# A new order of issue on TensorE, VectorE and ScalarE, from the state-space stage to the feed-forward

## The chip, the cores and the metric

The kernel runs on one core of one Trainium2 chip. The metric is the time of one execution on the device in microseconds (us). The core's engines each work through their own stream of instructions: TensorE (PE, matrix products, with its weight loads, PEld), VectorE (DVE), ScalarE (ACT), GpSimd (POOL) and SyncE (SP), which here issues most of the transfers. An engine takes its instructions in the order of its stream, and each instruction waits until what it reads is written and what it overwrites has been read.

## The reference

One layer of a hybrid encoder trunk, in float32, for 512 frames of a new stream and 64 next frames of a running one with a past of 256. The width is 1024. A state-space branch (Mamba-2, 8 heads) and a latent attention branch (8 heads) stand side by side; their outputs are joined, projected and added to x, and a SwiGLU feed-forward of width 2816 follows.

```python
def hybrid_layer(x, ckv_past, krope_past, ssm_h0, conv_buf, p):
    proj = rmsnorm(x, p['norm_mix']) @ p['w_in']       # z, xbc, dt, q, ckv
    ...
    xbc, conv_new = causal_conv(xbc, conv_buf, p['conv_w'], p['conv_b'])
    y, h_new = ssd_scan(xh, dt, A, Bm, Cm, ssm_h0)     # chunked state-space scan
    y_ssd = rmsnorm((y + d_skip * xh) * silu(z), p['ssd_norm'])
    ...
    o_lat = mla_attend(q_lat, q_rope, q_pos, keys_c, keys_r, ...)
    o = jnp.einsum('bthl,lhd->bthd', o_lat, p['w_uv']).reshape(b, T, MLA_WIDTH)

    x = x + jnp.concatenate([y_ssd, o], axis=-1) @ p['w_out']
    hf = rmsnorm(x, p['norm_ffn'])
    x = x + (silu(hf @ p['w_gate']) * (hf @ p['w_up'])) @ p['w_down']
    return x, c_kv, k_rope, h_new, conv_new
```

The layer is run for both streams with shared weights; the outputs are the normed x of both, the new keys, the states and the last rows of the convolution.

## The kernel before

All 576 frames (512 + 64) lie along the free axis, in two halves of 288. The layer's channels lie on the 128 partitions, eight tiles of them. A float32 product is made of three products of split operands, high x high, high x low and low x high: for each block of weights ScalarE casts a high part (`split_weights`, L127, tiles wh_...) and VectorE subtracts it to get the low part (L128, wl_...). Most matmuls are 128x128 weights by 288 columns.

The stages, in the order of time: the input projection and convolution; the state-space scan in chunks (`chunk_a`, `chunk_e`: L520 to L552 hold the decays, for which SyncE loads rows into the tile ecp); the keys' value block (`ps_v`, L657, copied to V by ScalarE at L658); attention by pairs of heads, whose last product is pv (`values`, L771); the output projection (`out_tile`), in eight tiles t and two halves, first for the state-space half (cat_y) and last for the attention half (cat_o, steps O0 to O7), with the result added to x2 by VectorE (`evac`, L802); then the feed-forward.

The feed-forward's products are made by a seven-product scheme on 2 x 2 blocks. For each block of gate, up and down weights, `block_weights` loads two halves r2 and r1 (SyncE, L898 and L899; tiles gu_0 and gu_1, or db_0 and db_1), makes sums of them on VectorE (L901 to L904), casts (ScalarE, L906), splits the results (L127, L128), and last takes a low part (VectorE, L912, gu_a). `block_product` (L945) multiplies; its results go to the banks ps_x, ps_y and ps_z. Steps of the feed-forward's elementwise work (L1022 to L1034) and the operands of the down product (L1058 to L1065) run on VectorE in between.

Which slot of a pool a tile gets is fixed by strings of digits (`PLACES`), so a load can start only when the last reader of the slot's former tile is done. The order of work on each engine is written out by hand: `ISSUE` has one list for each engine. The numbers count the engine's instructions in the order in which the program creates them; the place in the list is the order in which the engine gets them. `issue_in_order` (L1342) chains each entry to the one ahead of it:

```python
for name, text in ISSUE.items():
    made = [i for i in nc.cur_bb.bb.instructions if i.engine == engines[name].engine]
    order = list(_places(text))
    for a, b in zip(order, order[1:]):
        tc.add_manual_dep(made[b], made[a].name, info, reason="issue order")
```

The instructions that the text speaks of by number:

| list | number | instruction |
|---|---|---|
| PE | 875 | first product of a value block, ps_v (L657) |
| PE | 1390-1403 | fourteen of the last products pv (L771) |
| PE | 1388-1389 | last two products of ps_o6_1, out-projection of tile 6 (L465) |
| PE | 1404 | first product of ps_o0_0, step O0 (L465); same bank as ps_o6_0 |
| PE | 1900 | product ps_z of block 3 with wl_gu_S (L945) |
| DVE | 366, 367 | x2[6] plus ps_o6_0, plus ps_o6_1 (L802) |
| DVE | 368, 369 | low part of cat_o, 64 and 512 columns (L764) |
| DVE | 375, 377 | first sums gu_2 of the first gate-up block, of gu_0 and of gu_1 (L901, L903) |
| DVE | 482, 495 | low parts gu_a of blocks 3 and 4 (L912) |
| DVE | 481 | low part wl_gu_S of block 3 (L128) |
| DVE | 489, 491 | sums of block 4 (L902, L904) |
| DVE | 466, 467, 468 | operands of the down product, pv (L1059, L1060, L1061) |
| DVE | 469, 474 | down operand fz (L1065), sum u from ps_x (L1026) |
| DVE | 518 | first sum of the first down block, db_2 of db_0 (L901) |
| ACT | 127, 142 | copy V from ps_v (L658), exponential of ecp (L552) |

Of the kernel before, what the change touches and what calls it, by code (L numbers as in the profile page):

```python
# [1390 lines left out]
142-147 152-171 174 270-271 175-177 272-274 178-187 172-173 188-269 275-367 373-383 368-370 384-419 421 420 422-455  # L1391
469-470 371 456-461 372 471-473 462-468 474-575 577 576 578-588 613-619 657 620-622 589-591 623-627 637-639 658 640
628-633 592-595 641 634 659-660 596-597 635-636 598-607 665 608-612 653 666-693 661 713 765 694-712 714-716 642-644
717-723 645-652 737 724 761 725 762-763 738 764 726 739-742 727-728 743 729 744 831-832 730-735 745-748 736 749-753
833 754-756 769 834 757-758 770-775 759-760 776-796 662-664 797-813 654 814-816 655-656 835-837 817-824 766-768 872
890-892 869 838 893 829-830 873-874 825-827 894 828 878 870-871 879 895 863-866 875-877 880 855-862 881-887 867-868
926-929 888 930-931 889 898 839-840 899 841-842 900-905 843-845 906-909 846-853 910-911 854 912-921 938 896 939 897
932-934 940 922-925 941-943 935-937 947-956 993 957-960 944-946 994-995 1012-1013 996-1001 1014 977-980 961-962
981-984 963-976 985-992 1015-1017 1002-1007 1018-1019 1008-1011 1020-1022 1024-1025 1028 1026-1027 1023 1063 1051 1035
1029-1030 1039-1041 1064-1065 1052 1036 1053 1032-1034 1042-1043 1054 1044 1031 1037 1066-1067 1055-1056 1068-1070  # L1400
1057-1062 1071-1073 1048 1074 1049-1050 1077-1082 1091-1093 1038 1045-1046 1094-1102 1047 1107-1109 1075 1110-1111
1076 1112 1083-1090 1129-1132 1123-1124 1103 1125 1133 1104 1134-1137 1126-1127 1138-1140 1128 1113 1106 1114-1115
1105 1141-1147 1153-1155 1148-1152 1169-1170 1116 1171 1117-1118 1172-1177 1121 1163 1178-1180 1159-1160 1156 1164
1119-1120 1193-1204 1181-1188 1289-1290 1122 1189-1192 1167 1291-1293 1157-1158 1277-1284 1161 1294-1296 1285-1288
1297 1168 1298-1301 1162 1302-1304 1206 1205 1305-1306 1165 1313-1316 1307-1308 1317 1309 1207 1166 1310 1318 1208
1319-1322 1311 1224 1312 1209 1225 1227 1323-1324 1226 1218-1223 1210-1217 1253-1254 1228-1231 1325-1326 1241 1237
1327-1328 1242 1329 1232 1330 1337 1243 1331 1338 1233-1236 1238-1239 1250-1251 1339 1252 1340-1342 1240 1244-1245
# [7 lines left out]
1685 1659-1661 1680 1666 1678-1679 1669 1706-1708 1681 1709 1670 1689 1710-1711 1676 1695 1690 1682 1667 1686 1696
1704 1701 1698 1687 1697 1688 1691 1699 1712-1717 1692-1694 1705 1742-1748 1730 1718-1723 1700 1724-1726 1731
1727-1728 1732-1734 1729 1702-1703 1735-1736 1749 1737-1741 1750 1766 1751 1754-1756 1767 1757-1764 1752-1753
1768-1770 1765 1771-1777 1790-1801 1778-1779 1826 1780 1827-1832 1802 1781 1833-1835 1782-1784 1803 1850 1785 1851
1814 1836 1786 1815 1852-1853 1787 1816-1817 1854 1788 1818-1821 1837 1855 1804 1856 1789 1857-1859 1805-1806
1822-1824 1860 1807 1861 1808-1812 1825 1910-1913 1813 1886-1887 1862 1914 1863 1915-1916 1888-1889 1838 1917-1918  # L1420
1839-1847 1864 1848-1849 1865-1866 1919 1890 1920 1867 1891 1868 1921 1892 1869 1893-1896 1870 1897 1874-1876
1898-1899 1877 1922-1929 1871 1930-1932 1878-1880 1900-1907 1933 1908-1909 1872-1873 1881-1885 1946 1934 1947
1935-1939 1958 1948 1959-1961 1940-1942 1949 1943 1950 1944-1945 1951-1953 1962 1954-1957 1970 1963 1971-1972
1964-1969 1994 1973-1976 1982-1983 1977 1995 1978-1981 1984 2018 1985-1986 1996-1997 2072 1998-2000 1987-1990
2001-2002 2006 2003 2007 1991-1992 2008 2019 2073 1993 2020 2004 2021 2009-2010 2074-2075 2024 2076-2077 2011
2025-2026 2022-2023 2005 2102 2027-2028 2012-2014 2060 2103 2029 2061 2090 2104-2105 2015-2016 2091 2030 2062-2063
2048-2049 2017 2106-2107 2092-2096 2064 2031 2050-2053 2108 2032 2036 2109-2110 2037 2097 2065 2054 2038 2033-2035
2055 2039 2056 2066-2068 2111-2112 2098-2101 2113 2069-2070 2040-2041 2057-2059 2132-2133 2071 2114-2120 2042 2078
2121 2079 2043 2134 2084 2080 2044 2085 2122 2045 2123 2086-2089 2124 2081 2125 2046 2135 2082 2047 2126-2129 2083
2162-2164 2136-2137 2165 2130 2166 2138-2140 2131 2141-2145 2150 2146 2167-2168 2151 2147 2152-2155 2148-2149 2186  # L1430
2156-2160 2169-2171 2174 2161 2175-2177 2172 2178-2181 2187 2173 2192 2188 2182-2185 2189 2240-2244 2190-2191
2193-2194 2245 2204 2195-2197 2205 2198-2199 2228 2216 2206-2207 2258 2208-2210 2229 2211 2200 2217-2219 2230
2220-2222 2212 2259-2260 2201 2213-2215 2264 2261 2265-2266 2223 2262-2263 2231 2224-2225 2267 2232 2270-2272 2226
2234 2227 2276 2268 2282 2269 2235-2236 2283 2237 2284 2238 2285 2277-2278 2239 2279-2281 2286 2246 2287 2273 2247
2252 2274 2288 2248 2289 2249 2253 2202-2203 2275 2250-2251 2233 2294 2254 2290 2300 2291-2293 2255 2295 2301-2302
2296 2318 2303 2256 2330 2304-2306 2331 2307-2308 2319-2320 2309 2332 2310-2312 2321 2333 2257 2313 2334 2314 2322
2315 2323 2316 2335 2317 2336-2337 2324 2338 2325 2297 2354 2339-2340 2342 2326 2343 2355 2327 2344 2328-2329
2345-2351 2341 2366-2367 2356 2352 2357-2358 2368 2353 2359 2298 2369-2371 2360-2361 2299 2362 2378 2363-2364 2379
2365 2380-2381 2372 2382-2383 2373-2374 2384 2402 2375 2414-2415 2385 2390 2386 2416-2418 2391 2387-2388 2419 2403
2376 2392-2396 2404 2397 2420 2389 2398-2400 2405 2421-2422 2406 2401 2438 2423 2407-2409 2424 2410-2411 2377  # L1440
2412-2413 2425-2430 2439-2441 2450-2451 2442 2452-2453 2431-2433 2443 2434 2454 2435 2455 2436-2437 2456 2444-2446
# [247 lines left out]
```

## Time and profile before

| | |
|---|---|
| median of 3 runs | 636.05 us (635.5 to 636.56) |
| profiled execution | 636.12 us |
| its span, first to last instruction | 634.1 us |
| granted clock of TensorE, mean | 0.998 |
| TensorE busy | 621.4 us (98%), 4717 matmul records |
| VectorE busy | 552.4 us (87%), 979 instructions |
| ScalarE busy | 388.5 us (61%), 749 instructions |
| GpSimd busy | 73.2 us (12%), 112 instructions |
| DMA, mean over the span | 118 GB/s |

The profiled execution's span is 2.0 us shorter than its time: that lies ahead of the first and behind the last instruction. In a row of a timeline the first number is the start, the second the length, then engine, line, operation, what is written and read, the shape and a count; a bracket at the end gives the idle time ahead of it and what ended it. A row of waits names who waited for whom, the total in us, how often, and the longest.

### The profile page before, as it was taken

The numbers are of one execution on the slowest core, as the hardware profiler recorded it, in microseconds if no ns is written. First come the engines' busy times: TensorE is split into PE (matmuls) and PEld (weight loads), VectorE is DVE, ScalarE is ACT, GpSimd is POOL, SyncE is SP. The second block draws the span as 40 slices with busy tenths as digits, with TensorE's granted clock in tenths as the row PEclk, the third lists the DMA queues.
The fourth block names the chain that finished last, engine by engine and source line by source line (L and its number), as shares of the span: only waits on it lengthen the run. The fifth ranks groups of instructions, "written<-read, shape, count | busy, mean of one in ns | idle before, by whom it ended". The sixth has DMA issues, their size and how long they took to land.

```text
span 634.1 us, 12124 instructions
## 1 busy us (share of the span) xinstructions
PE 621.4 (98%) x4717; PEld 593.8 (94%) x4717; DVE 552.4 (87%) x979; ACT 388.5 (61%) x749; POOL 73.2 (12%) x112
## 2 busy tenths in 40 slices
PE   9999999999999999999999999999999999999995
PEld 8899999977897899999999899999999999999994
DVE  6999897799867599999998897889888998999775
ACT  7653536599857379855656465655564666635464
POOL 1321141001010000000011002100111011100032
PEclk9999999999999999999999999999999999999999
DMA  8622184414221231223267436551666255734105
GB/s 297 222 47 83 35 212 119 141 62 142 107 77 34 97 104 65 79 61 131 56 155 186 125 96 154 140 139 51 177 150 155 67 164 119 167 101 159 47 0 184
DMA packets 32889, 74.64 MB, mean 118 GB/s; under 512 B 3882, under 2 KB 11960, under 8 KB 32576
## 3 DMA queue, kind: packets, MB, share of 16 engines
q1 hardware_dynamic: 26688, 62.73, 30.6%
q0 software_dynamic: 5424, 10.57, 9.4%
q8 instruction: 37, 0.61, 0.4%
q10 hardware_dynamic: 720, 0.57, 0.3%
q14 instruction: 20, 0.16, 0.1%
HBM read 59.14 MB, written 4.15 MB: 100 GB/s over the span
## 4 chain that ended last, share of the span: by engine, by line
PE 86%; DMA 5%; DVE 4%; ACT 3%; issue 1%; SPq 0%; DVEq 0%; ACTq 0%
PE ps_x L945 20%; PE ps_z L945 10%; PE ps_dx L1085 9%; PE ps_in L143 8%; PE ps_o L465 5%; PE ps_y L945 5%; PE ps_dz L1085 4%; PE ps_l L1155 4%; PE sc L724 3%; PE ps_first L143 2%; PE ps_dy L1085 2%; PE ps_z L465 2%; DMA gu<-in_w_gu 2%; PE ps_p L945 2%; PE ptp L746 1%; PE pv L771 1%
## 5 line engine op out<-in xcount | busy, mean ns | idle before, releaser
L945 PE MATMUL ps_x<-xop,wh_gu_S 128*128 128x288 f32 x504 | 122.5, 295 | 0.0
L945 PEld LDWEIGHTS ps_x<-xop,wh_gu_S 128*128 128x128 f32 x504 | 87.0, 188 | 0.3 <-DVE u L1026 0.3
L945 PE MATMUL ps_x<-xop,wl_gu_S 128*128 128x288 f32 x252 | 73.7, 295 | 1.6 <-DVE wl_gu_S L128 1.6
L945 PE MATMUL ps_z<-xop,gu_a 128*128 128x288 f32 x252 | 61.7, 295 | 0.0
L127 ACT CAST wh_gu_S<-gu 128x1024 fp32r<-128x1024 f32 x44 | 46.0, 1053 | 15.2 <-PE ps_y L945 4.3
L128 DVE TENSOR_TENSOR wl_gu_S<-gu,wh_gu_S 128x1024 fp32r<-128x1024 f32 x44 | 53.0, 1219 | 0.9 <-ACT wh_gu_S L127 0.5
L945 PEld LDWEIGHTS ps_x<-xop,wl_gu_S 128*128 128x128 f32 x252 | 47.2, 188 | 1.8 <-DVE wl_gu_S L128 1.8
L1098 POOL DMA_DIRECT2D x<-db x16 | 14.8, 927 | 279.1 <-ACT dc L1091 169.5
L143 PE MATMUL ps_in<-xs,wh_in 128*128 128x288 f32 x256 | 45.5, 298 | 0.0
L945 PE MATMUL ps_y<-xop,wh_gu_A 128*128 128x288 f32 x168 | 44.7, 296 | 0.0
L945 PEld LDWEIGHTS ps_z<-xop,gu_a 128*128 128x128 f32 x252 | 43.5, 188 | 0.0
L945 PE MATMUL ps_x<-xop,wh_gu_A 128*128 128x288 f32 x168 | 42.9, 295 | 0.0
L945 PE MATMUL ps_z<-xop,wh_gu_S 128*128 128x288 f32 x168 | 42.1, 295 | 0.0
L143 PEld LDWEIGHTS ps_in<-xs,wh_in 128*128 128x128 f32 x256 | 37.8, 188 | 0.2
L127 ACT CAST wh_gu_A<-gu 128x1024 fp32r<-128x1024 f32 x22 | 23.1, 1050 | 16.7 <-PE ps_x L945 13.6
L128 DVE TENSOR_TENSOR wl_gu_A<-gu,wh_gu_A 128x1024 fp32r<-128x1024 f32 x22 | 26.8, 1219 | 4.2 <-ACT wh_gu_A L127 2.9
L945 PEld LDWEIGHTS ps_y<-xop,wh_gu_A 128*128 128x128 f32 x168 | 30.2, 188 | 0.1
L465 PE MATMUL ps_o<-cat_y,wh_out 128*128 128x288 f32 x128 | 29.9, 317 | 0.0
L945 PEld LDWEIGHTS ps_x<-xop,wh_gu_A 128*128 128x128 f32 x168 | 29.6, 188 | 0.0
L945 PEld LDWEIGHTS ps_z<-xop,wh_gu_S 128*128 128x128 f32 x168 | 29.2, 188 | 0.0
L143 PE MATMUL ps_in<-xs,wl_in 128*128 128x288 f32 x128 | 27.8, 296 | 0.0
L465 PE MATMUL ps_o<-cat_o,wh_out 128*128 128x288 f32 x128 | 27.4, 300 | 0.3 <-ACT ps_o L462 0.3
(609 smaller groups left out, 1997.2 us busy)
## 6 DMA issues: line engine op xcount, KB each, us to landing
gu<-in_w_gu SPq DMA_DIRECT2D x44, 512.0 KB, 4.9
db<-in_w_down SPq DMA_DIRECT2D x16, 512.0 KB, 3.9
x<-db POOLq DMA_DIRECT2D x16, 288.0 KB, 6.5
x<-dc POOLq DMA_DIRECT2D x16, 288.0 KB, 4.0
wr_in<-in_w_in SPq DMA_DIRECT2D x8, 512.0 KB, 6.3
wr_out<-in_w_out SPq DMA_DIRECT2D x8, 512.0 KB, 3.2
cumb<-cumD SPq DMA_DIRECT2D x5, 512.0 KB, 4.6
x<-in_xT SPq DMA_DIRECT2D x2, 1152.0 KB, 5.6
```

Source lines behind the costliest of these rows:

```text
L127: act.copy(hi, raw)
L128: dve.tensor_tensor(lo, raw, hi.bitcast(F32), ALU.subtract)
L143: pe.matmul(ps[:m, hf, :n], w, x[:, hf * n : (hf + 1) * n], start=start and k == 0 and i == 0, stop=stop and k == last and i == 2,)
L465: pe.matmul(ps[:, :n], w, x[:, cols], start=not onto and k == 0 and i == 0, stop=onto or (k == len(terms) - 1 and i == 2), skip_group_chec ...
L724: pe.matmul(s[:, :nk], qs[:, j, q0 : q0 + P], ks[:, j, :nk], start=True, stop=True)
L746: pe.transpose(pp[:, k : k + P], prs[p, i][:, j, b * P : b * P + P], ident)
L771: pe.matmul(pv[64 * j : 64 * j + 64, b * P :], V[b][:, h * HD : (h + 1) * HD], pts[p, b, j], start=b == 0, stop=True, skip_group_check=b > 0,)
L945: pe.matmul(ps, p, q, start=not onto and first and kp == kps[0] and j == 0, stop=onto or (last and kp == kps[-1] and j == 2), skip_group_c ...
L1085: pe.matmul(ps, l, r, start=not onto and k == 0 and j == 0, stop=onto or (k == n - 1 and j == 2), skip_group_check=onto,)
L1098: pool.dma_start(x2[t], v, accum_op=ALU.add)
L1155: pe.matmul(ps, w, x[:, cols], start=first and not onto and k == 0 and i == 0, stop=onto or (last and k == len(terms) - 1 and i == 2), ski ...
```

## The change

Only the lists `ISSUE["PE"]`, `ISSUE["DVE"]` and `ISSUE["ACT"]` are written anew. Those of GpSimd and SyncE stay, as do the instructions themselves, their operands, and the slots of `PLACES`. In the list of TensorE 1515 of 4431 places hold another instruction than before, in VectorE's 373 of 979, in ScalarE's 285 of 718; they run from 58 us (the end of the input projection) to 338 us (the first down blocks) of the profile. The lists are the same before and behind that. In each engine's stretch the same numbers occur, in another order.

```diff
     "PE": """
...
-1343 1332-1333 1246 1334-1336 1247 1276 1248-1249 1275 1263-1268 1255-1262 1269-1271 1366-1367 1272-1274 1368-1371
-1344 1349-1353 1355 1354 1345 1356 1346 1357-1358 1347 1372 1363-1364 1359-1361 1348 1365 1362 1373-1376 1378-1381
-1390-1403 1382 1377 1383-1389 1404-1486 1488-1489 1487 1490-1509 1629 1512 1510-1511 1513-1523 1632 1620 1524-1534
...
-1898-1899 1877 1922-1929 1871 1930-1932 1878-1880 1900-1907 1933 1908-1909 1872-1873 1881-1885 1946 1934 1947
...
+1276 1251-1252 1247-1249 1275 1263-1268 1255-1262 1269-1271 1366 1272 1347-1348 1367-1368 1273 1369 1274 1349-1351
+1370-1372 1352-1354 1373-1374 1355-1357 1375-1377 1358 1363-1365 1378-1380 1359-1362 1381-1387 1390-1403 1388-1389
+1404-1426 1428-1431 1427 1432-1496 1500 1497-1498 1501 1499 1502-1504 1632 1626 1505-1509 1512-1515 1510-1511
...
+1849 1862 1911-1919 1888-1892 1863-1865 1893-1896 1866 1897 1920-1921 1874-1877 1922-1931 1898-1899 1878-1883 1934
+1932 1884 1867-1869 1885 1870 1900-1903 1871 1904-1908 1872-1873 1935 1933 1936 1909 1937-1942 1946-1947 1943-1945
...
     "DVE": """
...
-335 328 327 339 337 336 331-332 342 338 345 361 343-344 340 351-352 346 349 353 341 347 354 348 350 363 362 365 364
-366 369 367 383 368 375 371 382 372 377 376 378-380 373 381 374 386 398 384 388 387 385 389 409 394 391 390 395
...
-453 440 460 452 441 477 459 479 442 478 488 476 463 435 462 443 480 465 464 473 490 470 482 474 495 467 466 481 489
-469 518 491 471 486 492 487 520 484 519 493-494 468 483 485 496-497 522 498 503 499 532 521 534 501 472 502 523 504
...
+350 363 362 365 364 375 377 366 368-369 367 383 371 380 372 382 378 376 379 373 381 386 390 374 398 384 388-389 387
...
+458 433-434 440 461 441 453 452 442 459-460 488 435 476 443 479 477 473 463 462 465 478 480 464 489 466 490 470 482
+474 518 495 467 491 468 481 492 484 494 469 483 487 486 485 520 499 497 493 471 496 519 498 503 501 522 504 500 521
...
     "ACT": """
...
-116 99 84 96 98 104 80 126 97 78 100 103 101 93 105 102 115 114 110 109 107 112 122 95 108 156 91 113 111 117 138 137
-163 106 140 135 141 139 119 121 128 142 136 123 134 143 127 120 208 129 124 130-132 152 147-148 154 151 145 157 133
...
+141 134 140 106 138 119 137 121 127 139 163 128 143 123-124 129 120 208 130-131 146 152 148-149 132 145 154 133 157
+150-151 147 142 125 144 210 155 153 158-159 162 160-161 118 168 164-165 170-171 166 178 172 179 169 167 184 174-175
...
```

More of the change, by code (lines that the diff above doesn't have):

```diff
@@ L1395 @@
[L1395 to L1404, printed above, removed]
@@ L1415 @@
[L1415 to L1419, printed above, removed]
@@ L1425 @@
[L1425 to L1429, printed above, removed]
@@ new lines @@
+1173 1154-1155 1174-1180 1121 1193 1167 1194 1181 1195-1196 1182-1183 1197-1203 1156 1122 1163 1184-1186 1204 1164
+1187 1157 1159-1161 1205 1289-1291 1162 1292-1294 1188 1168 1158 1295-1296 1189-1190 1165 1191-1192 1297-1300 1224
+1277 1207-1208 1278-1280 1209 1281-1282 1206 1166 1313 1283 1314-1315 1284-1287 1316 1288 1317-1319 1225 1301 1320
+1302-1307 1227 1321-1322 1308-1312 1323-1324 1226 1237 1218-1223 1210-1217 1253-1254 1228-1231 1236 1325-1326
+1232-1233 1327-1328 1337 1238-1239 1241 1240 1242-1243 1234-1235 1329-1335 1338-1341 1244-1246 1342-1346 1336 1250
@@ new lines @@
+1648 1584-1595 1653 1596-1604 1649 1608 1605 1643 1606 1609 1607 1668 1610-1619 1654-1655 1669 1638 1650-1652
+1662-1664 1645 1671 1656-1657 1646 1665 1674 1683-1684 1675 1685 1658 1639 1677-1678 1666-1667 1670 1689 1676 1690
+1706-1708 1672 1640 1679 1709-1710 1673 1695 1692 1659 1696 1691 1711-1714 1686 1704 1687 1715 1688 1716 1693
+1660-1661 1680 1717 1698-1699 1681 1700 1694 1682 1697 1705 1742 1718 1701 1743 1719-1721 1730 1744 1722-1724 1745
+1725 1746-1747 1731 1726-1729 1702 1732-1739 1703 1748-1751 1740 1752 1754 1741 1755-1756 1766 1753 1757-1765
@@ new lines @@
+2085 2118 2086-2087 2119-2120 2078-2080 2133 2121-2123 2044-2047 2088 2124 2134 2125-2127 2135-2136 2089 2081 2128
+2082-2083 2137-2140 2129-2131 2141-2144 2162 2150-2151 2145-2147 2163-2169 2240 2148-2149 2241 2152-2153 2170-2171
+2154-2155 2186-2187 2156 2242-2243 2157-2159 2188 2160-2161 2172 2244 2189 2245 2173-2180 2190 2181-2184 2192 2191
+2193 2185 2194-2196 2258 2270-2271 2197 2259 2198-2199 2216 2204-2208 2217 2222 2209-2211 2228 2212-2215 2223 2218
+2260 2219 2261-2262 2220-2221 2272 2200-2202 2229-2230 2263-2267 2224 2273 2234 2225 2235-2236 2282 2237-2238
@@ new lines @@
+2402 2375 2414-2415 2385 2390 2386 2416-2418 2391 2387-2388 2419 2403 2376 2392-2396 2404 2397 2420 2389 2398-2400
+2405 2421-2422 2406 2401 2438 2423 2407-2409 2424 2410-2411 2377 2412-2413 2425-2430 2439-2441 2450-2451 2442
+2452-2453 2431-2433 2443 2434 2454 2435 2455 2436-2437 2456 2444-2446 2457 2447-2448 2458 2449 2462-2466 2486 2459
+2467-2468 2474-2476 2469 2477 2470 2498 2460 2471-2472 2499 2487 2478-2479 2461 2500 2488 2480 2473 2501 2489-2490
+2481 2491-2492 2482 2493 2483 2494 2484 2495 2485 2502 2576 2522 2496 2577 2503-2505 2578 2497 2579-2580 2523-2524
@@ new lines @@
+2510 2525 2581 2506-2507 2511-2512 2526-2527 2513-2514 2528 2606 2515 2529 2516-2519 2530 2520-2521 2531 2564 2607
+2532-2533 2508 2534 2509 2535 2540 2565 2541 2608 2566 2594 2552 2542 2536 2567 2600 2543-2545 2601 2553 2568 2595
+2554-2555 2569 2596 2546-2547 2597 2537 2548 2558 2549 2556 2550 2598-2599 2609 2538 2557 2602 2551 2559 2539 2603
+2560-2561 2610-2611 2562-2563 2618 2570-2571 2619 2572 2604 2573 2612 2574-2575 2605 2582-2583 2613 2620 2614-2617
+2588 2630-2632 2621 2589 2622 2590 2633 2623-2624 2584-2587 2636 2625 2637 2634 2626-2627 2638 2591 2628-2629
@@ new lines @@
+2639-2640 2654-2657 2592 2658 2642-2643 2593 2641 2635 2644-2645 2659-2661 2646 2666 2647-2649 2667 2662 2650
+2663-2665 2668 2651-2652 2669 2653 2670 2690 2671-2672 2696-2697 2673 2691 2698 2678 2674 2679-2680 2675 2681-2685
+2692 2676-2677 2686-2687 2744 2699-2700 2688-2689 2745-2747 2701-2702 2693-2695 2748 2708-2711 2703 2712-2713 2726
+2714 2727 2749 2732 2715 2704 2733-2734 2716 2720 2717 2721 2705 2722-2723 2762 2718 2774 2763 2724 2706 2728 2725
+2764 2729 2719 2768 2735 2765 2769 2775 2730 2738 2766 2739 2731 2740 2776-2777 2707 2741-2742 2786 2743 2770 2767
@@ new lines @@
+2906-2907 2894-2895 2918 2889 2908-2909 2919 2890-2892 2910 2896-2898 2911 2879-2880 2899 2893 2900 2912-2913
+2901-2902 2914 2881 2903 2915 2904-2905 2920 2916 2921-2923 2917 2942-2943 2924 2930-2935 2944-2945 2936 2954 2925
+2955 2926 2946-2947 2937 2948 2927 2938 2928-2929 2956 2949-2951 2939 2952 2940 2953 2957 2941 2958-2963 2978
+2964-2969 2990 2970-2971 2979 2972-2975 2980 2976-2977 2981 3002 2982 2991 2983 3003 2992 3004 2984 2993-2995 2985
+2996 3005 2997 2986 2998 3006 3080 2999-3001 3007 3081 3008 2987 3082 2988 3009 3026-3028 2989 3029 3010-3011 3083
@@ new lines @@
+3390 3413 3391-3392 3414 3384 3398 3393-3394 3415 3395 3422 3396 3423 3399 3424 3416 3397 3400 3425 3401 3417
+3402-3405 3446 3418 3406 3426 3447 3407-3408 3427-3430 3419 3385 3420 3409 3448-3449 3421 3431-3433 3450-3453
+3434-3437 3454 3438-3439 3458 3455 3440-3442 3456-3457 3459 3443-3445 3460-3464 3482 3465 3506 3466 3470 3467
+3471-3472 3483 3473 3468 3474-3476 3507 3494 3477 3484 3495 3478 3508 3479-3481 3485 3496 3486-3487 3469 3488 3497
+3489-3492 3498-3499 3493 3500 3509 3530 3501 3510 3502 3531 3511 3518 3503 3519-3520 3504 3512 3532 3584 3521 3513
@@ new lines @@
+3522 3505 3585 3514 3523-3524 3533 3515 3534 3525 3535 3586 3526 3516 3587 3527 3536 3517 3528 3588 3529 3589 3537
+3572 3538 3573 3539-3541 3560 3574 3542 3548 3602 3549 3543-3544 3561-3562 3545 3550-3551 3603-3604 3563 3552-3553
+3614 3564-3565 3615 3554-3557 3546 3575 3547 3608 3578 3566 3576-3577 3567 3609 3579 3605 3558 3568 3616 3610
+3569-3570 3559 3571 3580 3617 3606 3618 3581-3582 3607 3611-3612 3590 3626 3591 3583 3592 3627 3620 3613 3621
+3593-3594 3622 3628 3623 3629 3624-3625 3630 3595 3638 3631 3639 3596 3619 3632-3633 3640-3641 3597 3634-3636
@@ L1518 @@
+4319 4337-4338 4320-4321 4339-4340 4323 4341 4324 4342 4325 4343 4326 4344 4327 4371 4359 4328-4329 4348-4349 4345
+4330-4331 4358 4350 4383-4384 4351 4372 4352-4353 4332 4354 4360 4333 4355 4361 4373-4374 4385 4356 4375-4376 4395
+4357 4386 4396 4387-4388 4362-4363 4389 4364 4397 4365-4366 4377-4378 4367 4379 4398 4368 4399 4380 4369 4390 4400
+4391 4401 4370 4392 4381 4393 4382 4394 4402 4407 4403-4406 4408-4430
 """,
@@ L1552 @@
+947 946 948-949 951 956 952 950 954-955 953 958 960-961 964-965 957 959 962 966 963 967-978
 """,
@@ L1578 @@
+713-714 717 716 715
 """,
```

268 lines of the change are left out of this document (118 added, 150 removed).

## The prediction

> **What bounds the kernel now.** I read the page's busy times first, then TensorE's waits in the stretch whose order changes (58.7 to 338 us), then its windows, and last the timelines around the few places that stood out.
>
> ```profile
> span 634.1 us, 12124 instructions
> PE 621.4 (98%) x4717; PEld 593.8 (94%) x4717; DVE 552.4 (87%) x979; ACT 388.5 (61%) x749; POOL 73.2 (12%) x112
> ```
>
> ```profile
> PE ps_v L657 <- ACT V L658: 1.5, 1, 1.5
> PE ps_o L465 <- ACT ps_o L462: 0.3, 1, 0.3
> PE ps_p L945 <- ACT xop L877: 0.2, 1, 0.2
> ```
>
> ```profile
> 90.00:145.00 55.00, 53.48 (x473) 48.28 (x472) 45.33 (x88) 36.86 (x94) 9.44 (x13) 1.00 0.38 110
> ...
> 218.00:262.00 44.00, 43.52 (x317) 42.18 (x316) 41.68 (x73) 35.20 (x62) 0.00 (x0) 1.00 0.33 116
> 262.00:338.00 76.00, 76.00 (x574) 76.00 (x574) 74.79 (x121) 47.10 (x80) 4.41 (x5) 1.00 0.36 102
> ```
>
> TensorE is busy 98% of the span; in the changed stretch it waits three times, 2.0 us in all. That is the ceiling of any gain, since the diff moves instructions and removes none. The columns are the stretch, its length, the busy time of TensorE, its weight loads, VectorE, ScalarE and GpSimd with their instructions, the granted clock, and the share and rate of the DMA. The last stretch has no idle TensorE at all, and gives its cadence: 76.00 us for 574 matmuls, 0.132 us each. VectorE is nearly as full: 74.79 of 76.00 us. So what a new order on VectorE makes wait, it can't catch up soon, and TensorE has no slack of its own to give.
>
> **How the lists are read.** VectorE has 979 recorded instructions and its list 979 entries, so the n-th row is the n-th entry; the numbers below were put on the rows so. An engine stands at an entry until its inputs are there. What counts is therefore where an entry that needs a late input now stands ahead of one that TensorE needs.
>
> **Part 1: the state-space stage.** One wait of 1.5 us, at the first product of a latent value block:
>
> ```profile
> 126.19 0.63 ACT L552 ACTIVATE ecp<-ecp 128x512 f32<-128x512 f32 x1 [1.79 <-DMA ecp<-cumD]
> 127.68 0.57 ACT L658 COPY V<-ps_v 128x512 f32<-128x512 f32 x1
> 128.30 0.50 PE L657 MATMUL ps_v<-wh_uv,ckv 128*128 128x512 f32 x1 [1.52 <-ACT V L658]
> ```
>
> ScalarE stands 1.79 us for a load into ecp, with the copy V queued five instructions behind it; TensorE needs that copy. The new ScalarE list has the copy (127) at place 130 instead of 136 and the exponential of ecp (142) at 154 instead of 131, so the copy no longer stands behind the load. The wait goes, 1.5 us. What is late next: the new lists put TensorE's ps_v ten places earlier and the first out-projection product five places earlier, against inputs that come when they came. Bounds: nothing is won (a wait of the same size moves on), or 2.0 with every small wait gone. I take 1.5 less three earlier matmul places that nothing covers, 3 x 0.132 = 0.4, since 0.132 each is the nearest row: **-1.1**.
>
> **Part 2: the attention stage's end and the first gate-up block.** VectorE's list read `365 364 366 369 367 383 368 375 371 382 372 377`; it now reads `365 364 375 377 366 368 369 367 383 371 380`. 366 adds the finished ps_o6_0 to x2 (L802) and so empties its bank; 375 (L901) and 377 (L903) are sums for the first gate-up block, of the loads issued at L898 and L899. TensorE's product 1404, the first of O0, writes the bank that 366 empties.
>
> ```profile
> 217.33 0.46 DVE L802 TENSOR_TENSOR x<-ps_o,x 128x288 f32<-128x288 f32 x1 [3.19 <-PE ps_o L465]
> 219.98 0.69 DVE L901 TENSOR_TENSOR gu<-gu 128x512 f32<-128x512 f32 x1
> 221.92 0.68 DVE L903 TENSOR_TENSOR gu<-gu,gu 128x512 f32<-128x512 f32 x1
> ```
>
> ```profile
> 216.75 0.41 PE L465 MATMUL ps_o<-cat_y,wh_out 128*128 128x288 f32 x1
> 216.99 0.43 PE L465 MATMUL ps_o<-cat_y,wl_out 128*128 128x288 f32 x2
> 218.06 0.42 PE L465 MATMUL ps_o<-cat_o,wh_out 128*128 128x288 f32 x2
> ```
>
> ```profile
> 216.21 0.33 SPq L898 DMA_DIRECT2D gu<-in_w_gu  x1
> 216.59 0.43 SPq L899 DMA_DIRECT2D gu<-in_w_gu  x1
> ```
>
> ```profile
> SPq L898 <- PE pv L771: 20.5, 1, 20.5
> ```
>
> ```profile
> 220.03 0.62 ACT L906 CAST gu_a<-gu 128x512 fp32r<-128x512 f32 x1 [2.58 <-DMA gu<-in_w_gu]
> ```
>
> ```profile
> gu<-in_w_gu SPq DMA_DIRECT2D x2, 512.0 KB, 4.2
> ```
>
> SyncE waits 20.5 us for the last product pv, whose operand lies in the place that the load fills; in the new TensorE list seven of the nine products of ps_o6 that stood between pv (1390-1403) and O0 go ahead of pv, two stay behind it. TensorE's work ahead of O0 is the same, but pv, and with it the load, comes 7 x 0.13 nearer to O0. I keep pv's end, so 216.21, as the fixed point. ScalarE, which stood 2.58 us for it, starts at 220.03: it lands at about 220.0. The median of both from issue to landing is 4.2; with 3.8 for the first, the second took 4.6 and lands at 216.59 + 4.6 = 221.2. Then: 375 from 220.0 to 220.7; 377 from 221.2 to 221.9 (its 0.68); 366 starts 0.08 before that end, as rows behind each other do, and takes 0.46: 222.3, with 0.05 to TensorE 222.33. TensorE, which had nine matmuls from 216.75 to 218.06, now has two to do behind pv and is ready for O0 at 216.75 + 0.24 + 0.13 = 217.12. A wait of **+5.2**, where there was none (O0 began at 218.06, straight behind the nine). Bounds: 0.6 less if the second load takes the first one's 3.8 (377 then starts behind 375), and 0.8 more if it takes that spread longer than reckoned: 4.6 to 6.0. Behind 366 on VectorE stand 368, 369 (the low part of cat_o, due ten matmuls into O0, 1.3 us) and 367; they end within 1.0 us of 366 and cost nothing.
>
> **Part 3: between the two blocks.** The other two waits of the view, 0.3 and 0.2, lie in the moved stretch behind O0, and TensorE's delay there lets the copies that it waited for finish: **-0.5**. Bounds: 0 and -0.5.
>
> **Part 4: the first down block.** VectorE's list read `482 474 495 467 466 481 489 469 518 491`; it now reads `489 466 490 470 482 474 518 495 467 491 468 481`. 482 (L912) is the last reader of a buffer that the first load for down goes to; 518 (L901) is the first sum of that load; 481 (L128) makes the low part of the weights S3 and S4 of block 3, which TensorE's product 1900 reads.
>
> ```profile
> 283.12 0.69 DVE L912 TENSOR_TENSOR gu_a<-gu,gu_a 128x512 fp32r<-128x512 f32 x1
> 283.72 0.46 DVE L1026 TENSOR_TENSOR u<-ps_x,u 128x288 f32<-128x288 f32 x1
> 284.24 0.69 DVE L912 TENSOR_TENSOR gu_a<-gu,gu_a 128x512 fp32r<-128x512 f32 x1
> 284.85 0.45 DVE L1060 TENSOR_TENSOR pv<-u,pv 128x288 f32<-128x288 f32 x1
> 285.22 0.45 DVE L1059 TENSOR_TENSOR pv<-u,u 128x288 f32<-128x288 f32 x1
> 285.59 1.22 DVE L128 TENSOR_TENSOR wl_gu_S<-gu,wh_gu_S 128x1024 fp32r<-128x1024 f32 x1
> 286.73 0.69 DVE L902 TENSOR_TENSOR gu<-gu,gu 128x512 f32<-128x512 f32 x1
> 287.70 0.69 DVE L901 TENSOR_TENSOR db<-db 128x512 f32<-128x512 f32 x1
> 288.30 0.68 DVE L904 TENSOR_TENSOR gu<-gu,gu 128x512 f32<-128x512 f32 x1
> ...
> 295.27 0.45 DVE L1061 TENSOR_TENSOR pv<-u,pv 128x288 f32<-128x288 f32 x1
> ```
>
> ```profile
> 283.87 0.38 SPq L898 DMA_DIRECT2D db<-in_w_down  x1
> ```
>
> ```profile
> SPq L898 <- DVE gu_a L912: 14.1, 1, 14.1
> ```
>
> ```profile
> db<-in_w_down SPq DMA_DIRECT2D x1, 512.0 KB, 3.7
> ```
>
> ```profile
> 288.57 0.29 PE L945 MATMUL ps_z<-xop,wl_gu_S 128*128 128x288 f32 x1
> ```
>
> The load leaves 0.07 behind the end of 482 (283.80) and lands 3.7 later. In before, the seven instructions from 474 to 469 cover that, and 518 starts at 287.70 without a wait. Now only 474 (0.46) stands between, so VectorE stands some 3.3 us. From the end of 482 to that of 481: 3.81 to the landing, then 518, 495, 467, 491, 468 and 481 by the distances of their rows, 0.60 + 0.61 + 0.37 + 0.60 + 0.37 + 1.22, together 7.58. Before it was 286.81 - 283.80 = 3.01. So 481 is later by 4.57, and by 0.97 more since 489 (0.60) and 466 (0.37) now stand ahead of 482. TensorE reads it five matmuls later, -0.66, and had slack: 288.57 - 286.81 less 0.05 is 1.71. That leaves 3.2; VectorE's little idle ahead (1.2 of 76 us) takes up some 0.3: **+2.9**. Bounds: 0.3, if TensorE read it ten matmuls later instead of five and all of VectorE's idle (1.2) and both moved sums (0.97) were hidden; 3.7, the whole landing.
>
> **Part 5: the rest.** About 1500 other entries of TensorE, 340 of VectorE and 280 of ScalarE change places. The same instructions run; what hides them is the 0.132 cadence of TensorE with its inputs ready, as the stretch from 262 to 338 shows. Price if that cover goes: as the waits above. I take 0, with 1 us either way for the range. From 338 us on all lists are the same. SyncE's and GpSimd's lists don't change, but SyncE's two loads stand as reckoned above.
>
> **The sum.** -1.1 + 5.2 - 0.5 + 2.9 = +6.5. The profiled execution took 636.12 us (span 634.1 and 2.0 around it), 0.07 above the median of 636.05, so 642.6 against that execution and **642.5 us** against the median.
>
> **The rivals.** The first: after standing for 5 us TensorE runs slowly for a while.
>
> ```profile
> 1.06 3.78 PE L218 MATMUL ps_warm<-ones 128*128 128x128 f32 x16 [1.06 <-POOL nepsb L110]
> 5.32 2.07 PE L143 MATMUL ps_first<-xs,wh_first 128*128 128x288 f32 x9 [0.47 <-ACT xs L157]
> ```
>
> At the start nine matmuls go from 5.32 to 7.23, 0.212 each against 0.132. A share of 0.38 is lost, over 1.9 us of this row alone or 6.2 from the first matmul: 0.7 to 2.3. I take 1.9, once, behind wait 2 (the other is shorter): **644.4 us**. For it: the start. Against it: no idle of TensorE in this stretch is over 1.5 us, and the one at 128.30 lies in a stretch (90 to 145) with a clock of 1.00, so these rows can't decide. The Trainium skill, "TensorE: Matmul & The Clock Gate", section "Why this matters for your kernels", states that a gap of more than some 3 us between bursts takes the clock to half; by that rule it would happen behind wait 2, while for wait 4 the gap is too near to say.
>
> The second: only one of the two waits appears. Wait 2 alone (the down load lands under cover, VectorE being so late that the load is there): 636.05 - 1.6 + 5.2 = **639.6**. Wait 4 alone (366 isn't what O0 needs first): 636.05 - 1.6 + 2.9 = **637.3**.
>
> The third, on the other side: VectorE reaches 375 so late that both loads have landed, because it is behind by the time it leaves 364, and likewise at 518. Then only the early gain stays: 636.05 - 1.6 = **634.4**. It decides if VectorE comes to 375 after 221.2 instead of some 214; that is 7 us of delay, of which the rows show none: VectorE stood 3.19 us idle ahead of 366. The fourth: the lists don't tell in time, since TensorE had only 2.0 us to lose and inputs come early enough: 636.
>
> **How the numbers follow.** Both waits, as summed: 0.50, own range 640.5 to 644. Slow clock behind them: 0.20. Wait 2 alone 0.08, wait 4 alone 0.06. Faster 0.10, no change 0.06. About 0.2%, 1.3 us, is what a measurement can tell from no change: faster is under 634.8, slower over 637.3. Wait 4 alone lies on that edge and is halved: same 0.09, slower 0.81, faster 0.10. Leaving out the two fastest cases, 0.16, the range begins at 637.0; it ends at 646.0, the forecast with the clock's 2.3 and 1.2 of the upper bounds above (0.8 and 0.8, not both in full).
>
> **What would show it.** Wait 2: a row of L802 on VectorE behind the two sums, idle on a load at the first, and a TensorE wait of ps_o on x (L802) of 5 us. Wait 4: VectorE idle of 3 us ahead of the first db sum, and a TensorE wait on wl_gu_S (L128) of 3 us. Part 1: no wait on V. The clock: a granted clock under 1.00 in the window behind wait 2. Wrong would be the sum if pv came earlier against the rest, or if the landing of either load were shorter by more than a microsecond.

## The result, and the profile after

The changed kernel takes 647.08 us (median of 6 runs, 644.91 to 647.5) against 636.05 us (6 runs, 635.5 to 636.56): a ratio of 1.0167, interval 1.0152 to 1.0182. That is 11.0 us slower, where 6.5 had been forecast and 646.0 was the end of the range. The profiled execution took 646.19 us, 10.1 more than the one shown of before, with a granted clock of 0.991 instead of 0.998.

The busy times of the page of after, and TensorE's waits from 50 to 350 us (who waited for whom, total, times, longest):

```profile
span 644.3 us, 12133 instructions
PE 624.5 (97%) x4717; PEld 594.9 (92%) x4717; DVE 553.9 (86%) x979; ACT 388.2 (60%) x749; POOL 72.9 (11%) x112
```

```profile
PE ps_o L465 <- DVE x L802: 5.2, 1, 5.2
PE ps_z L945 <- DVE wl_gu_S L128: 2.8, 1, 2.8
PE ps_b L536 <- DVE bc L413: 1.1, 1, 1.1
PE ps_y L573 <- ACT R L640: 0.3, 1, 0.3
PE ps_z L465 <- DVE zh L476: 0.2, 1, 0.2
```

The two large waits are those that the prediction reckoned at 5.2 and 2.9 us; they came out at 5.2 and 2.8. The wait on V is gone, and three that before did not have stand in its place. But TensorE is also busy for 3.1 us more with the same 4717 records. The windows of after show where (length, TensorE, weight loads, VectorE, ScalarE, GpSimd; the third number from the end is the granted clock):

```profile
218.00:224.00 6.00, 0.85 (x9) 0.44 (x4) 1.95 (x5) 1.06 (x2) 0.00 (x0) 0.94 0.73 262
224.00:226.00 2.00, 2.00 (x9) 2.00 (x10) 2.00 (x3) 2.00 (x3) 0.00 (x0) 0.50 0.01 4
226.00:228.00 2.00, 2.00 (x14) 2.00 (x14) 1.00 (x3) 0.04 (x1) 0.00 (x0) 0.82 0.00 0
...
296.00:298.00 2.00, 0.00 (x0) 0.00 (x0) 2.00 (x4) 1.38 (x2) 0.00 (x0) 1.00 0.01 4
298.00:300.00 2.00, 1.98 (x9) 1.98 (x10) 2.00 (x3) 0.49 (x1) 0.00 (x0) 0.60 0.00 0
300.00:302.00 2.00, 2.00 (x11) 2.00 (x10) 1.43 (x3) 0.22 (x2) 0.00 (x0) 0.55 0.76 231
302.00:304.00 2.00, 2.00 (x17) 2.00 (x16) 1.59 (x4) 0.95 (x3) 0.00 (x0) 1.00 0.73 293
```

Behind each of the two waits the clock falls to about half, for some 3 us: nine to eleven matmuls in 2 us instead of fifteen. The first wait in the timelines of after, VectorE's rows, SyncE's load and TensorE's rows:

```profile
221.46 0.69 DVE L901 TENSOR_TENSOR gu<-gu 128x512 f32<-128x512 f32 x1 [6.21 <-DMA gu<-in_w_gu]
222.74 0.69 DVE L903 TENSOR_TENSOR gu<-gu,gu 128x512 f32<-128x512 f32 x1 [0.60 <-DMA gu<-in_w_gu]
223.35 0.45 DVE L802 TENSOR_TENSOR x<-ps_o,x 128x288 f32<-128x288 f32 x1
```

```profile
217.64 0.33 SPq L898 DMA_DIRECT2D gu<-in_w_gu  x1
```

```profile
218.41 0.29 PE L465 MATMUL ps_o<-cat_y,wl_out 128*128 128x288 f32 x1
223.86 0.85 PE L465 MATMUL ps_o<-cat_o,wh_out 128*128 128x288 f32 x2 [5.15 <-DVE x L802]
224.51 0.44 PE L465 MATMUL ps_o<-cat_o,wl_out 128*128 128x288 f32 x1
224.75 0.68 PE L465 MATMUL ps_o<-cat_o,wh_out 128*128 128x288 f32 x2
```

VectorE stands 6.21 us for the load that left at 217.64, then 0.60 for the second; only then does it empty the bank (L802), and TensorE stands 5.15. From 224.51 to 224.75 one matmul takes 0.24 where the cadence was 0.132. The second wait:

```profile
290.20 0.45 DVE L1026 TENSOR_TENSOR u<-ps_x,u 128x288 f32<-128x288 f32 x1
294.20 0.69 DVE L901 TENSOR_TENSOR db<-db 128x512 f32<-128x512 f32 x1 [3.55 <-DMA db<-in_w_down]
...
296.75 1.22 DVE L128 TENSOR_TENSOR wl_gu_S<-gu,wh_gu_S 128x1024 fp32r<-128x1024 f32 x1
```

```profile
298.02 0.40 PE L945 MATMUL ps_z<-xop,wl_gu_S 128*128 128x288 f32 x1 [2.84 <-DVE wl_gu_S L128]
```

VectorE stands 3.55 us for the down load behind 474 (L1026), as reckoned (3.3), and 481 comes five rows behind.

### The profile page after: what moved, and what is told of

It is laid out like the page before. It is cut to its first block, busy times and chain, and to the rows that moved or that the text cites. A ratio compares the mean times of both kernels' runs of the same rounds, so it can differ in the third digit from the quotient of the medians.

```text
span 644.3 us, 12133 instructions
## 1 busy us (share of the span) xinstructions
PE 624.5 (97%) x4717; PEld 594.9 (92%) x4717; DVE 553.9 (86%) x979; ACT 388.2 (60%) x749; POOL 72.9 (11%) x112
## 4 chain that ended last, share of the span: by engine, by line
PE 83%; DVE 8%; DMA 5%; ACT 2%; issue 1%; POOL 0%; SPq 0%; DVEq 0%; POOLq 0%; ACTq 0%
PE ps_x L945 17%; PE ps_z L945 9%; PE ps_dx L1085 9%; PE ps_o L465 8%; PE ps_in L143 6%; PE ps_dz L1085 4%; PE ps_y L945 4%; PE ps_l L1155 4%; PE ps_z L465 3%; PE sc L724 3%; PE ps_first L143 2%; PE ps_dy L1085 2%; DMA gu<-in_w_gu 2%; PE ps_p L945 2%; PE ptp L746 1%
## 5 line engine op out<-in xcount | busy, mean ns | idle before, releaser
L465 PE MATMUL ps_o<-cat_y,wh_out 128*128 128x288 f32 x128 | 32.5, 328 | 0.0
L945 PE MATMUL ps_z<-xop,wl_gu_S 128*128 128x288 f32 x84 | 25.2, 301 | 2.8 <-DVE wl_gu_S L128 2.8
```

Source lines behind the costliest of these rows:

```text
L465: pe.matmul(ps[:, :n], w, x[:, cols], start=not onto and k == 0 and i == 0, stop=onto or (k == len(terms) - 1 and i == 2), skip_group_chec ...
L945: pe.matmul(ps, p, q, start=not onto and first and kp == kps[0] and j == 0, stop=onto or (last and kp == kps[-1] and j == 2), skip_group_c ...
```

## The experiments

Each kernel differs from before or after by list entries, except where a diff shows code. Times stand beside runs of before on the same chip, whose median differs by a microsecond from chip to chip; so ratios are compared.

**Sums put back.** Two kernels from the changed lists, and one with both edits:

```diff
 DVE, e1_sums_back
-375 377 366 368 369 367 383 371
+366 368 369 367 383 375 377 371
 DVE, e2_down_back
-482 474 518 495 467 491 468 481 492
+482 474 495 467 491 468 481 518 492
 DVE, e3_both_back: both
```

> The changed lists with the sums 375 and 377 put back behind the four x2 and cat_o entries (366 368 369 367 383 375 377). Theory (each wait costs itself and a stretch at half clock behind it): the 5.2 us wait on x (L802) goes and with it twelve matmuls at 0.24 instead of 0.132, 1.3 us; 647.1 - 6.5 = 640.6, the wait of 2.8 on wl_gu_S and its slow stretch stay, clock 1.00 in the whole stretch from 216 to 262. Rival (the waits alone carry the loss, the slow clock is a coincidence of the stage): 647.1 - 5.2 = 641.9, with a clock under 1.00 behind O0 still. Second rival (VectorE has to stand for the load anyway and the wait only moves to a later entry): over 644, with a new TensorE wait on VectorE between 219 and 235 us.

> The changed lists with 518, the first sum of the down load, put back behind 481. Theory: the wait of 2.8 on wl_gu_S goes, and with it fifteen matmuls at 0.24 instead of 0.132, 1.6 us; 647.1 - 4.4 = 642.7, the wait of 5.2 stays. Rival (waits alone): 647.1 - 2.8 = 644.3. Second rival (the stand of VectorE moves to 518's new place and makes 492 or 484 late for TensorE): 645 or more, a wait on wl_gu_A or on g.

> Both put back. Theory: 647.1 - 6.5 - 4.4 = 636.2, so the other 2100 moved entries together bring nothing (the wait on V gone, 1.5, against 1.1 + 0.3 + 0.2 of new ones in the state-space stage). Rival (my prediction's early gain of 1.6 is there and something else of the lists costs the rest): 634.5. Clock 1.00 throughout.

Measured: e1 644.36 us, ratio 1.0131 (1.0104 to 1.0158); e2 643.03, 1.0114 (1.0091 to 1.0137); e3 640.08, 1.0068 (1.0043 to 1.0093). e2 lies nearer to the theory (wait and slow clock, 642.7) than to the waits alone (644.3), but its interval holds both; its profile decides, with no wait on wl_gu_S and the clock at 1.00 from 226.45 us to the end of TensorE's work. e1 is the second rival's case, and e3 fell outside both forecasts, for the same reason. TensorE's waits of e3:

```profile
PE ps_o L465 <- DVE x L802: 2.2, 1, 2.2
```

```profile
224.01 0.53 PE L465 MATMUL ps_o<-cat_y,wh_out 128*128 128x288 f32 x2 [2.17 <-DVE x L802]
```

The edit left 371 behind the sums, and 371 empties the bank that O1 needs, as 366 empties that of O0. So the wait moved to the next bank and kept 2.2 us: every entry behind a late input inherits it, and putting back the first is not enough.

**The sums alone, in the old lists, and the stand filled with work.**

```diff
 DVE of before, e4_sums_ahead
-366 369 367 383 368 375 371 382 372 377
+375 377 366 369 367 383 368 371 382 372
 e7_filled (32) and e12_half_filled (19), on top of it, ahead of O0 in out_tile and in PE's list
+        if hfs == (1,) and t == 0:
+            for _ in range(32):
+                pe.matmul(last_sc[0][:, :TH], wk(w, 0)[0], cat_y[0][0][:, :TH], start=True, stop=True)
```

> The lists of before with only 375 and 377 put ahead of 366. In before nine matmuls stand between pv and O0 instead of two, so the wait should be 222.33 - 218.06 = 4.3 us. Theory: 4.3 and 1.3 for the slow clock, 636.1 + 5.6 = 641.7. Rival (waits alone, no slow clock behind a wait in this list): 640.4. Second rival (the loss needs the rest of the new lists): within 1 us of 636.

> The lists of before with 375 and 377 ahead of 366, and 32 additional matmuls of 128x128 by 288 (their result is not used) between 1389 and O0, 32 x 0.132 = 4.2 us, so that TensorE works while it would stand 4.4. Theory (the stand itself makes the clock fall to half): the end of the wait is set by the second load and 366 and stays where it is, the idle time shrinks to 0.2, the clock stays 1.00 and O0's matmuls run at 0.132: 641.8 - 1.3 = 640.5 although more work is done. Rival (the slow matmuls belong to this place or to the transfers of that moment): 641.8, clock 0.5 behind O0. Second rival (the added work delays pv or the loads): over 642.

> As e7_filled, with 19 additional matmuls instead of 32, so that TensorE stands 4.4 - 19 x 0.132 = 1.9 us. An idle time of 1.6 was followed by the full clock (at 354 us in before), one of 2.2 by a short stretch at half. If what counts is idle time over some 2 us: full clock behind the wait and the time of e7_filled, 638.8 or 2.5 over before. If half clock comes from 1.6 on: ten matmuls at 0.24, 1.1 more.

Measured: e4 641.79 us, 1.0101 (1.008 to 1.0123), against 641.7 expected; e7 638.82, 1.0036 (1.0021 to 1.0051), under the 640.5 expected; e12 639.83, 1.005 (1.0029 to 1.007), which holds the 2.5 us over before that were expected if the clock stays up. O0's first rows on TensorE, of e4, e7 and e12:

```profile
222.67 0.85 PE L465 MATMUL ps_o<-cat_o,wh_out 128*128 128x288 f32 x2 [4.40 <-DVE x L802]
223.31 0.45 PE L465 MATMUL ps_o<-cat_o,wl_out 128*128 128x288 f32 x1
223.55 0.69 PE L465 MATMUL ps_o<-cat_o,wh_out 128*128 128x288 f32 x2
```

```profile
218.39 4.37 PE L807 MATMUL sc<-cat_y,wh_out 128*128 128x288 f32 x32
222.81 0.53 PE L470 MATMUL ps_o<-cat_o,wh_out 128*128 128x288 f32 x2
223.18 0.29 PE L470 MATMUL ps_o<-cat_o,wl_out 128*128 128x288 f32 x1
223.31 0.43 PE L470 MATMUL ps_o<-cat_o,wh_out 128*128 128x288 f32 x2
```

```profile
223.82 0.54 PE L470 MATMUL ps_o<-cat_o,wh_out 128*128 128x288 f32 x2 [1.71 <-DVE x L810]
224.19 0.29 PE L470 MATMUL ps_o<-cat_o,wl_out 128*128 128x288 f32 x1
```

O0 starts at the same moment in e4 and e7 (222.67 and 222.81), but in e7, with 32 more matmuls ahead of it, it runs at the full cadence: adding useless work made the kernel faster. So the slow stretch comes from TensorE's standing, and not from the place or its transfers. With 1.71 us of idle time left (e12) the clock stays up too. In the profiles e7's span is 2.1 us under e4's (637.3 and 639.4); 1.4 of it is the clock, and 0.7 a smaller wait on wl_gu_S at 354 us. The medians, on two chips, stand further apart than that.

**The down sum alone, in the old lists.**

```diff
 DVE of before, e5_down_ahead
-482 474 495 467 466 481 489 469 518
+482 474 518 495 467 466 481 489 469
```

> The lists of before with only 518 put ahead, straight behind 474. From the end of 482 to that of 481: 3.81 + 0.60 + 0.61 + 0.37 + 0.37 + 1.22 = 6.98 instead of 3.01; less the 1.71 of slack a wait of 2.3 us on wl_gu_S. Theory: 2.3 and about 0.9 for a short slow stretch, as behind the wait of 2.2 of e3_both_back: 635.8 + 3.2 = 639.0. Rival (waits alone): 638.1. Second rival (VectorE's stand is caught up): within 1 us of 635.8.

639.58 us, 1.0047 (1.0028 to 1.0066): the theory's 639.0, 3.2 over its before, lies within, and so do the waits alone, 2.3 over. The rows decide, with a wait of 2.4 as reckoned and matmuls at 0.24 us from 292.34 on:

```profile
291.35 0.40 PE L945 MATMUL ps_z<-xop,wl_gu_S 128*128 128x288 f32 x1 [2.37 <-DVE wl_gu_S L128]
...
292.34 0.45 PE L945 MATMUL ps_z<-xop,wl_gu_S 128*128 128x288 f32 x1
292.58 0.45 PE L945 MATMUL ps_z<-xop,wh_gu_S 128*128 128x288 f32 x1
```

Fourteen matmuls from 292.34 to 295.65 took 3.31 us instead of 1.85: the slow stretch cost 1.5 us, more than the 0.9 expected.

**Where the early gain went.** New lists up to a place, old ones from there (e6 to O0, e13 to the end of the state-space stage), the reverse (e14), pv's place alone (e11), and the changed kernel with both blocks in order (e8):

```diff
 PE of before, e11_pv_late
-1390-1403 1382 1377 1383-1389
+1382 1377 1383-1387 1390-1403 1388-1389
 DVE of after, e8_both_as_before (and 518 as in e2)
-375 377 366 368 369 367 383 371 380 372 382 378 376 379
+366 369 367 383 368 371 375 372 377 380 382 378 376 379
```

> The new lists only up to O0 (place 1404 of TensorE, 367 of VectorE, 277 of ScalarE), the old ones from there. Theory (the early part wins the 1.5 us wait on V and loses it to new waits: ScalarE now stands for the load of cumb with the copies bt and R behind it, and VectorE's bc runs long beside GpSimd's select): 635.8 + 0.4 = 636.2, between 635 and 637.5. Rival (my prediction's early gain of 1.1 is there): 634.7. Second rival (the early lists carry the 3.5 that e3_both_back kept): 639.

> The new lists only up to the end of the state-space stage (place 940 of TensorE, 223 of VectorE, 166 of ScalarE), the old ones from there. My prediction's early gain of 1.1 was placed here. Theory (the wait on V goes, and the waits on bc and on R come, of a size that changes from run to run): 636.3 + 0.2 = 636.5, between 635.5 and 637.5, so no gain. Rival (the stage gains 1.1 as predicted, and the early loss of e6_early_only is all in the attention stage and at O0): 635.2.

> The lists of before with only seven products of ps_o6 (1382, 1377, 1383-1387) put ahead of the last products pv (1390-1403), as the new list of TensorE has it. Theory (the loads of the first gate-up block leave at the end of pv, so they land 7 x 0.132 = 0.9 later against the rest; 375 stands 0.9 for them with 371 behind it, and 371 had 0.2 of slack before O1): a wait of 0.7 on x (L802), 636.2 + 0.7 = 636.9. Rival (VectorE takes it up): within 0.3 of 636.2.

> The changed lists, with VectorE's order at the first gate-up block 366 369 367 383 368 371 375 372 377 380, so that 371, which empties the bank of the next product, stands ahead of the sums too (in e1_sums_back and e3_both_back it stood behind them and TensorE waited 2.3 there), and 518 back behind 481. Theory: no wait over 1.6 is left and no slow stretch: 640.1 - 2.2 - 0.9 = 637.0. Rival (the rest of the new lists costs by itself): 639 or more. Second rival (all else is neutral): 636.

> The old lists up to O0 (places 1404, 367, 277) and the new ones from there: the counterpart of e6_early_only. Theory (the parts add): the wait on x is 4.4 as in e4_sums_ahead, since pv stands where it stood, with 1.3 of slow clock; the wait on wl_gu_S 2.8 with 1.6; the small waits of 0.5 go: 636.3 + 9.6 = 645.9. Rival (the two waits need the early lists' lateness): under 643.

| | us | ratio to before | interval |
|---|---|---|---|
| e6_early_only | 638.22 | 1.0026 | 1.0014 to 1.0038 |
| e13_ssd_only | 636.01 | 0.9998 | 0.9987 to 1.0009 |
| e11_pv_late | 637.36 | 1.0013 | 1.0001 to 1.0025 |
| e8_both_as_before | 638.67 | 1.0031 | 1.0018 to 1.0045 |
| e14_late_only | 644.45 | 1.0135 | 1.0116 to 1.0154 |

The state-space stage brings nothing (e13). Its waits on TensorE from 50 to 350 us no longer hold V, but:

```profile
PE ps_b L536 <- DVE bc L413: 1.1, 1, 1.1
PE ps_y L573 <- ACT R L640: 0.6, 1, 0.6
PE ps_p L945 <- ACT xop L877: 0.3, 1, 0.3
```

R is the load wait in a new place: in the new list ScalarE stands for cumb (L520) with R queued behind it, as it stood for ecp with V behind (ScalarE of e13):

```profile
127.51 0.22 ACT L520 ACTIVATE hcw<-cumb 128x8 f32<-128x8 f32 x1 [0.83 <-DMA cumb<-cumD]
...
128.88 0.22 ACT L640 COPY R<-ps_g 128x64 f32<-128x64 f32 x1
```

These waits change in size: in the seven traces with the new lists of this stage (after, e1, e2, e3, e6, e8, e13) TensorE's rows from 58 to 140 us take between 0.8 us less and 1.0 us more than in before.

pv's new place, seven matmuls nearer to O0, costs 0.8 us (e11; 0.1 to 1.6 by its interval), with one new wait, since the load leaves later and 371 stands behind 375:

```profile
222.41 0.53 PE L465 MATMUL ps_o<-cat_y,wh_out 128*128 128x288 f32 x2 [1.05 <-DVE x L802]
```

e6 costs 1.7 by its ratio, and 638.22 lies over the 635 to 637.5 that were expected. 0.8 of it is pv's place, nothing the state-space stage; the rest lies in the attention stage, where no wait on TensorE is over 0.1 us. By the timelines the same rows, from 140 us to O0, take some 0.7 us longer there, in after, e6 and e8 alike. 0.6 of it lies at the 64 score products (L724), which take 15.2 us instead of 14.5 from each start to the next row's; what in the order of matmuls does it was not tried. e8 keeps 2.0 for the same reasons, so it did not go back to before, and its theory (637.0) was too low. e14, 1.5 us under its expectation in the median (which its interval still holds), has both waits:

```profile
PE ps_o L465 <- DVE x L802: 4.2, 1, 4.2
PE ps_z L945 <- DVE wl_gu_S L128: 2.7, 1, 2.7
```

But behind its second wait the clock stays up. The windows around that wait, two of after and then three of e14, cut where the granted clock can change:

```profile
294.97:298.38 3.41, 0.57 (x4) 0.36 (x3) 3.41 (x6) 1.38 (x2) 0.00 (x0) 1.00 0.01 3
298.38:301.80 3.42, 3.42 (x17) 3.42 (x16) 3.05 (x5) 0.69 (x1) 0.00 (x0) 0.50 0.41 122
```

```profile
292.34:295.75 3.41, 2.50 (x19) 2.26 (x18) 2.00 (x4) 0.63 (x1) 0.00 (x0) 1.00 0.64 247
295.75:299.16 3.41, 1.59 (x12) 1.59 (x13) 3.41 (x6) 1.49 (x3) 0.00 (x0) 1.00 0.01 2
299.16:302.57 3.41, 3.41 (x27) 3.27 (x26) 3.41 (x7) 1.84 (x4) 0.00 (x0) 1.00 0.75 243
```

In all sixteen traces the granted clock changes only on a grid of steps of 3.41 us, counted from its first rise to full (at 4.84 us in after, at 5.62 in e14). In after the whole wait of 2.84 us falls into one step, in which TensorE works for 0.57 us, and the next step is at half. In e14 the wait of 2.73 us lies across two steps, with 0.91 and 1.82 us of idle time, and no step behind it is slow. e14's first wait, on the other hand, was followed by two slow steps: 23 matmuls from 222.02 to 227.62 lost 2.6 us, where one step had been expected to cost 1.3.

e6's 1.7 (1.0026) and e14's 8.6 (1.0135) add up to 10.3, of the whole's 10.6 (1.0167) on 636. That they fit so well is partly luck, since the clock cost e14 2.6 us behind one wait and after 3.0 us behind two.

**What was worth keeping.**

```diff
 ACT of before, e9_copy_ahead
-128 142 136 123 134 143 127 120 208
+128 127 136 123 134 120 142 143 208
 DVE, e10_two_waits, besides
-589 575 591 582 571 556 581
+589 575 582 581 591 571 556
```

> The lists of before with only ScalarE's copy V (127), with 136, 123, 134 and 120, put ahead of the exponential of ecp (142) and of cumb's (143). Theory (the part of the change that was right: the copy doesn't need the load it stands behind): the wait of 1.5 on V goes and no new one over 0.3 comes: 636.2 - 1.4 = 634.8. Rival (the exponential is late next, and E or the state sum waits for it instead): within 0.4 of 636.2, a new wait between 128 and 135 us.

> As e9_copy_ahead, and on VectorE the two wl_gu_S (582, 581) put ahead of 591, which waits 1.7 us for a load at 350.31. Theory: the wait of 1.6 at 354.36 goes too: 636.2 - 1.4 - 1.4 = 633.4. Rival (wl_gu_S waits for ScalarE's cast there, and the wait only shrinks): 634.2 to 634.8.

e9 takes 635.15 us, 0.9976 (0.9963 to 0.9989), and e10 633.87, 0.9951 (0.9938 to 0.9965): faster than both kernels. In e9 the copy V waits for its own product and the exponential runs without a wait behind it:

```profile
125.63 0.58 ACT L658 COPY V<-ps_v 128x512 f32<-128x512 f32 x1 [1.06 <-PE ps_v L657]
...
127.07 0.65 ACT L552 ACTIVATE ecp<-ecp 128x512 f32<-128x512 f32 x1
```

What remains in e10's view of TensorE from 50 us on:

```profile
PE ps_p L945 <- ACT xop L877: 0.9, 1, 0.9
PE ps_v L657 <- ACT V L658: 0.4, 1, 0.4
```

The wait on wl_gu_S at 354 us is gone in e10's profile, but it is gone in e9's too, where its order wasn't touched (it changes between runs). So e10's second edit is likely a gain (0.9951 against 0.9976), but the intervals overlap at their ends.

## Why the prediction was wrong in size

The direction and both mechanisms were right, and the two waits came out as worked out by hand: 5.2 and 5.15, 2.9 and 2.84. Moved into the old lists one by one they cost what the rows say (e4, e5), and there the first was 4.4, since nine matmuls stood behind pv, as the same sum gives. What failed is the clock, left out of the sum, and the gain of part 1.

**The clock.** It was priced as a rival, 1.9 us "once, behind wait 2", at 0.20, and left out of the sum, where it stood at 0. Both waits were followed by half clock. Behind the first twelve matmuls took from 223.86 to 226.82, 2.96 us instead of 1.58: 1.4. Behind the second sixteen took from 298.02 to 301.74, 3.72 instead of 2.11: 1.6. Together 3.0, and e7 shows that the standing causes it. The start rows had the right cost (0.38 lost over 2 to 6 us: 0.7 to 2.3 for each wait); it was wrong to take it once, and to hold it unlikely, since the one idle time shown, 1.5 us, says nothing on 5. The Trainium skill, "TensorE: Matmul & The Clock Gate", section "Why this matters for your kernels", warns of gaps over some 3 us; by that rule it would have been in the forecast for wait 2. The measured waits do not fit one length of wait: 1.71 us (e12) and 2.73 (e14) left the clock at 1.00, while 2.17 (e3), 2.37 (e5) and 2.84 (after) did not, and the measurement decides. What fits all sixteen traces is the idle time within one step of 3.41 us: a step at full clock was followed by one at half whenever TensorE stood 1.97 us or more within it (the least, in e2), and never when it stood 1.82 us or less (the most, in e14). So that the clock fell behind wait 4 too hung on where that wait lay in the steps, which the rows of before could not tell.

**Part 1.** -1.1 was taken for the state-space stage; e13 measured 0 (0.9998, -0.8 to +0.6 us). In the changed kernel TensorE was ready for O0 at 218.54 instead of 218.06 although it had been 0.26 ahead of before where the lists begin to differ: +0.7. By 140 us it was still 0.20 ahead, so nearly all of that is lost in the attention stage, which the prediction held under part 5 at 0. "A wait of the same size moves on" was named as a bound, with 1.1 chosen from the wait that goes. It should have been chosen by asking of the new list which load stands ahead of which copy there: it was cumb, ahead of R. The wait of 1.1 on bc, which also stands against the gain, was not foreseen either.

**Part 3** was -0.5. From O0's end to 262 us the distance to before shrinks from 7.2 to 5.9 us, more than reckoned; the two waits account for 0.5, and the rest was not tried. **Part 5**'s 0 held behind 338 us, where the two traces stay 10.4 apart, within 0.3 to the end; ahead of O0 it did not (the 0.7 of the attention stage), though that lies within the 1 us that it allowed.

The sum with the measured terms: +0.7 + 5.2 + 1.4 - 1.3 + 2.8 + 1.6 = 10.4, against 10.1 between the profiled executions, of which the changed one had been 0.26 ahead at the start of the stretch. Of the other rivals none occurred: both waits came, and VectorE had no lateness that would have hidden the loads.

## What to carry to other kernels

In a hand-written order, an entry that needs a transfer must not stand ahead of an entry that the busiest engine needs; reckon its place from the instruction that lets the transfer start, and ask of every entry behind it when its reader is due. Moving the entry by one place too few only moves the wait (e1). A wait of TensorE over 2 us can cost more than itself: reckon a stretch at half clock behind each as a case of its own, here 1.4 to 2.6 us lost, and nothing where the wait was spread over two steps of the clock, with at most 1.82 us in one (e14). A wait removed is a gain only after the new list has been searched for the next one of its kind.

## What the runs showed of the hardware

TensorE's granted clock changed only in steps of 3.41 us. It fell to half for one step, or for two (e2, e14), behind a step in which TensorE had stood 1.97 us or more. So a wait of only 2.17 us took it down (e3) when it lay within one step, and one of 2.73 us (e14) did not when it lay across two. Filling the idle time with unused matmuls kept the clock up and made the kernel faster (e7 against e4).

VectorE's short bc (L413), 0.21 us elsewhere, took 1.73 beside GpSimd's two selects on cumb, and ended with them (timelines of after):

```profile
94.80 1.73 DVE L413 SCALAR_TENSOR_TENSOR bc<-cth,cacc 128x64 f32<-128x64 f32 x1
```

```profile
94.40 2.05 POOL L545 TENSOR_SCALAR_AFFINE_SELECT cumb<-cumb 64x512 f32<-64x512 f32 x2
```

In e2, where only one select ran at that time, to 95.20, the same instruction took 0.67. That is the new wait of 1.1 on bc, and it comes and goes between kernels whose lists are the same there. The Trainium skill, "GPSIMD Engine Reference", section "Specifications", states that the two engines share their way to SBUF and contend when a VectorE instruction has two SBUF inputs; bc has two, and the trace agrees.
